# A head's value products and sums issued at the end of its own step, with priority

## The chip, the cores and the metric

The kernel runs on one core of one Trainium2 chip. The metric is the device time of one execution in microseconds (us), as the median of several runs. Names of engines: PE (TensorE, matrix products), DVE (VectorE), ACT (ScalarE), POOL (GpSimd), SP (issues DMA transfers).

## What is computed

Two layers over 512 latent tokens and 256 context tokens of width 1024, all in 32-bit floating point. Layer 0 mixes the tokens by 16 heads of attention over all 768 tokens, layer 1 by 16 heads whose latent keys are a neighbourhood of the query on a grid (and all context tokens). Behind each mixer stands a mixture of 32 experts, of which every token uses two.

```python
def attend(q, k, v):
    s = jnp.einsum('bhgqd,bhkd->bhgqk', q, k, preferred_element_type=jnp.float32)
    p = jax.nn.softmax(s, axis=-1).astype(v.dtype)
    return jnp.einsum('bhgqk,bhkd->bhgqd', p, v)

for l in range(DEPTH):                       # DEPTH = 2
    h_l = modulate(x_lat, norm_mix[l], sh1, sc1)
    h_c = modulate(x_ctx, norm_mix[l], sh1c, sc1c)
    o_c, o_l = mixer_ab(...) if l % 2 == 0 else mixer_na(...)
    x_lat = x_lat + g1 * o_l
    ...
    y = hier_moe(tokens, moe_w_rg[l], ...)   # the same for the context in layer 0
    x_lat = x_lat + g2 * y
return rmsnorm(x_lat, norm_final)
```

The shifts, scales and gates come from a product of the conditioning with w_ada, the "modulation".

## The kernel before

The time divides into four parts: projections and heads of layer 0 (27.6 to 471.3 us of the profiled execution), its experts (to 1184.7), projections and heads of layer 1 (to 1491.9), and the experts and the end (to 2108.9). The change is about the two parts with heads; the heads themselves, from the transposes of the first head's maxima on, take 164.8 to 468.5 us in layer 0 and 1264.2 to 1487.1 in layer 1.

Scores are kept transposed: a score tile holds 128 keys by 512 queries, so that its exps can be the right operand of the product with the values. In layer 0 a head has six such tiles (512 latent queries) and, on two of them, one of 128 keys by 256 context queries. Eight heads are "stacked" (a score tile takes two products, L340 and L341), eight take three (L343 to L345). In layer 1 a head has two tiles of context keys (cunit) and four of latent keys with up to 384 queries each (lunit). Before the exp the maximum of each query is subtracted: it is found a head ahead, by products and DVE reductions of their own (L286, L292 and DVE L288, L293 in layer 0; L303, L313 and DVE L307, L314 in layer 1), negated (L321, L323), transposed into a row (L326, L332) and copied by ACT into a row of the Q operand (L328, L333).

Behind the exp (ACT L356 and L361, in layer 1 L400 behind a DVE addition of the bias, L398) a tile goes two ways. The value products (L421, L425; in layer 1 L432, L438) use the exps as they are; an output of 64 columns takes half of the array, so that the products of the two halves of the queries (hf 0 and 1) run beside each other. The adds sum the exps of all tiles into acc: on POOL for tiles 1, 2 and 4 in layer 0 and for tiles c1 and 1 in layer 1, otherwise on DVE (L371 to L374, L406). When acc is whole, four products with a one-hot operand (L453, 32 columns wide, one per group of queries, beside each other) give the sums over the keys in ps_sum. At the end ACT copies the value sums into oT (L459), and a batch of heads is divided by its sums (norm_units: L491, L493).

The order is set by run_heads (L497 on). Its step i hands over, for j from 0 to 5: score tile j of head i, the maxima of head i + 1, value unit j of head i - 1, in layer 1 a piece of the projections of later heads (the filler, L1840, for i up to 12), and the add of tile j - 1; the sums of head i - 1 stand at j = 4, its ACT copy at the step's end. Step n does the value products of the last head. In layer 0 prep0 (L963, L978, L990) makes values and queries of heads to come, and extra0 calls ada_pump, that is one step of the modulation (L139: 16 products of 32 columns). A scheduler then orders each engine's instructions: it takes the order of handing over as priority and moves an instruction forward where those ahead of it aren't ready in its own model. An engine executes its list in order.

PSUM buffers: score tiles use two (ps_s), maxima and projections two (ps_a) and in layer 0 a third (ps_v); value sums are also in ps_v, sums in ps_sum. A 32-bit product is recorded twice in the trace.

## Time and profile before

| | us |
|---|---|
| median of 3 runs | 2105.77 (2102.83 to 2112.57) |
| profiled execution, its own time | 2110.64 |
| its span, first to last instruction | 2108.9 |
| PE busy | 1878.8 (89%) |
| DVE busy | 789.5 (37%) |
| ACT busy | 656.6 (31%) |
| POOL busy | 321.3 (15%) |

The mean granted clock of PE is 0.957 of full speed. The busy shares are means over parts with different limits: the experts' parts move up to 414 GB/s from memory, the parts with heads 134 and 85 GB/s on the mean. A row of the timeline has the start, the duration, the engine, the line, the operation, the names (out<-in) and shapes, and how many like it follow one another; a bracket at its end says how long the engine was idle before it and which instruction released it. PE's products overlap, so that the distance between two starts says more about the price of one than its duration.

### The profile page before, as it was taken

To read this page: it belongs to the slowest core of one execution; us is meant where nothing else is said; L and a number is where in the kernel's file an instruction comes from. 1 tells how busy PE (TensorE), PEld (TensorE's weight loads), DVE (VectorE), ACT (ScalarE), POOL (GpSimd) and SP (SyncE) were. 2 spreads that over 40 slices of the span, in tenths; PEclk is the share of its full clock that TensorE was granted. 3 is DMA by queue.
4 is the path that set the end of the run, shared out by engine and by line. 5 is a ranking of instruction groups with operands and counts; after the bars stand their busy time and mean duration, and the time that the engine had idled before them with its cause. 6 is when DMAs were issued, how large, how long until landed. Compare 5 with 4: busy or idle time off the path is not lost. (4 is left out here: it accounts for less than half of the span.)

```text
span 2108.9 us, 29478 instructions
## 1 busy us (share of the span) xinstructions
PE 1878.8 (89%) x10307; PEld 1043.7 (49%) x10308; DVE 789.5 (37%) x2041; ACT 656.6 (31%) x1462; POOL 321.3 (15%) x313
## 2 busy tenths in 40 slices
PE   7999999989969999999996999999878999978983
PEld 5886555647833333333332887676663333322321
DVE  4656676557831111111113637666760000000003
ACT  4335643442211111111112526655423222212212
POOL 0002222121011111111110101111201111111100
PEclk9999999999979999999998999999988999999997
DMA  9655321014679999699996512223578999999995
GB/s 378 217 194 209 137 94 51 5 41 158 217 296 413 414 416 380 273 390 413 414 417 242 206 43 85 73 74 132 219 269 335 412 414 414 414 414 411 413 400 191
DMA packets 96736, 563.64 MB, mean 267 GB/s; under 512 B 17446, under 2 KB 18266, under 8 KB 42928
## 3 DMA queue, kind: packets, MB, share of 16 engines
q1 hardware_dynamic: 81520, 527.41, 63.3%
q0 software_dynamic: 14912, 32.19, 4.2%
q8 instruction: 189, 3.10, 0.6%
q14 instruction: 115, 0.94, 0.1%
HBM read 543.20 MB, written 33.23 MB: 273 GB/s over the span
## 5 line engine op out<-in xcount | busy, mean ns | idle before, releaser
L1522 DVE TENSOR_TENSOR hTe<-hTe,ps_s 128x256 f32<-128x256 f32 (+1 forms) x74 | 29.9, 405 | 399.0 <-ACT hTe L1521 281.9
L1503 ACT ACTIVATE gu<-ps_a 128x512 f32<-128x512 f32 x64 | 38.2, 597 | 441.0 <-PE ps_v L1537 387.4
L1543 DVE SCALAR_TENSOR_TENSOR y<-ps_v,tg,g 128x512 f32<-128x512 f32 x32 | 24.0, 751 | 392.1 <-PE ps_v L1537 392.1
L1498 PE MATMUL ps_a<-A,xT 128*64 128x512 f32 x544 | 151.5, 602 | 5.4 <-DMA A<-in_we_dram 2.0
L1537 PE MATMUL ps_v<-wp,hTe 128*64 128x512 f32 (+1 forms) x496 | 118.0, 547 | 18.7 <-PEq L1570 17.0
L1498 PE MATMUL ps_a<-wp,xT 128*64 128x512 f32 x496 | 127.4, 594 | 1.0
L1484 ACT ACTIVATE xT<-ps_m,mods,ab 128x64 f32<-128x64 f32 x256 | 79.2, 417 | 137.9 <-PE ps_m L1477 137.9
L1544 POOL DMA_INDIRECT ybuf<-y,tab x64 | 64.7, 1012 | 330.7 <-DVEq L1583 225.4
L1840 PE MATMUL ps_v<-hT,B 128*128 128x512 f32 x384 | 102.7, 396 | 0.0
L1537 PE MATMUL ps_v<-wE,hTe 128*64 128x512 f32 (+1 forms) x352 | 90.2, 566 | 9.6 <-PEq L1570 9.6
L1498 PEld LDWEIGHTS ps_a<-A,xT 128*64 128x64 f32 x544 | 50.8, 138 | 86.9 <-issue 72.6
L356 ACT ACTIVATE pt<-ps_s 128x512 f32<-128x512 f32 x96 | 57.3, 597 | 115.1 <-PE ps_s L345 73.3
L1434 POOL DMA_INDIRECT A<-hbuf,tab x41 | 42.1, 1027 | 293.7 <-PE ps_m L1477 227.2
L1498 PEld LDWEIGHTS ps_a<-wp,xT 128*64 128x64 f32 x496 | 44.3, 137 | 72.6 <-issue 66.6
L1498 PE MATMUL ps_a<-we,xT 128*64 128x512 f32 x288 | 76.2, 595 | 3.7 <-DMA we<-in_we_dram 2.4
L1498 PE MATMUL ps_a<-wf,xT 128*64 128x512 f32 x256 | 73.7, 597 | 2.5 <-PEq L1586 0.7
L1840 PEld LDWEIGHTS ps_v<-hT,B 128*128 128x128 f32 x384 | 68.4, 188 | 12.2 <-issue 1.9
L1434 POOL DMA_INDIRECT x<-hbuf,tab x33 | 33.8, 1026 | 261.1 <-PE ps_m L1477 222.2
L1537 PEld LDWEIGHTS ps_v<-wp,hTe 128*64 128x64 f32 (+1 forms) x496 | 34.0, 129 | 73.1 <-issue 68.8
L1498 PE MATMUL ps_a<-wE,xT 128*64 128x512 f32 x240 | 64.7, 618 | 1.4 <-ACT xT L1484 0.5
L1498 PE MATMUL ps_a<-B,xT 128*64 128x512 f32 x224 | 58.9, 595 | 3.4 <-DMA B<-in_we_dram 2.4
L1537 PE MATMUL ps_v<-we,hTe 128*64 128x512 f32 x144 | 47.6, 654 | 15.8 <-PEq L1570 15.8
(556 smaller groups left out, 3816.6 us busy)
## 6 DMA issues: line engine op xcount, KB each, us to landing
wp<-in_we_dram SPq DMA_DIRECT2D x106, 1024.0 KB
A<-in_we_dram SPq DMA_DIRECT2D x84, 1024.0 KB
wE<-in_we_dram SPq DMA_DIRECT2D x62, 1024.0 KB
we<-in_we_dram SPq DMA_DIRECT2D x54, 1024.0 KB
wslot<-in_w_ada_dram SPq DMA_DIRECT2D x23, 2048.0 KB
B<-in_we_dram SPq DMA_DIRECT2D x40, 1024.0 KB
wf<-in_we_dram SPq DMA_DIRECT2D x38, 1024.0 KB
qkE<-in_wqk_dram SPq DMA_DIRECT2D x8, 1024.0 KB
```

The source lines that it names most:

```text
L356: act(h.PT[i], ps, AF.Exp, scale=h.scale)
L1434: return nc.gpsimd.indirect_dma_start(out=dst, out_offset=None, in_=S.hbuf.rearrange("n (q f) -> (n q) f", q=2), in_offset=bass.IndirectOf ...
L1484: act(xT[:, k, :], pv[:, k % 4, k // 4, :], AF.Identity, scale=ab[l][:, 1, k, 0:1], bias=mods[l][:, 24 + k, 0:1])
L1498: mm(ps[M * g:M * g + M, :N], xT[:, 4 * h + k, :M], w[:, (g * N) // 512, k, f:f + N], start=(h == 0 and k == 0), stop=(h == 1 and k == 3))
L1503: act(out[-1][:, :N], ps[:, :N], AF.Copy)
L1522: V.tensor_tensor(hv, hv, pv[:, 1], op=OP.mult)
L1537: mm(ps[M * g:M * g + M, :N], hT[:, c, :], wd[:, c, g * N:g * N + N], start=(c == 0), stop=(c == 3))
L1543: V.scalar_tensor_tensor(y[:, :N], ps[:, :N], gates[0], g2[0], op0=OP.mult, op1=OP.mult)
L1544: st = nc.gpsimd.indirect_dma_start(out=S.ybuf.rearrange("n (q f) -> (n q) f", q=n // 2), out_offset=bass.IndirectOffsetOnAxis(ap=idx, axi ...
L1840: mm(ps[:, :n], wqk[:, j, b, k, :], hT[:, a, k, c0:c0 + n], start=(k == 0 and i == 0), stop=(k == 7 and i == 2))
```

## The change

Four things change. In run_heads the loop has n steps, and the value products, the sums and the ACT copy of head i (no longer of head i - 1) are handed over at the end of step i, under `tc.high_priority()`: the scheduler takes them ahead of all else that is ready. In av_units the order of the value units is turned: layer 0 begins with tile 5, layer 1 with tiles 1 and 3, then 0 and 2, then the rest of 2 and 1, then the context tiles; the flags that start and stop the accumulation move with them. In score_units the two score tiles of the context queries go from steps 0 and 1 to steps 2 and 3, their add to step 3. In ada_pump the modulation step has high priority too. Lines below are numbered anew: 421 is 422 after, 425 426, 432 433, 438 439, 453 454, 374 375, 493 494, 963 966, 1840 1843.

```diff
--- before.py
+++ after.py
@@ -354,11 +354,11 @@
                 mm3(ps, h, i * 128, 256, 512)
                 h.PT[i] = pp.tile([128, 512], F32, name="pt", bufs=8)
                 act(h.PT[i], ps, AF.Exp, scale=h.scale)
-                if i < 2:
+                if i in (2, 3):
                     ps = P("s")
-                    mm3(ps, h, i * 128, 0, 256)
-                    h.PT["c", i] = pp.tile([128, 256], F32, name="ptc", bufs=4)
-                    act(h.PT["c", i], ps[:, :256], AF.Exp, scale=h.scale)
+                    mm3(ps, h, (i - 2) * 128, 0, 256)
+                    h.PT["c", i - 2] = pp.tile([128, 256], F32, name="ptc", bufs=4)
+                    act(h.PT["c", i - 2], ps[:, :256], AF.Exp, scale=h.scale)
 
             def two(x):
                 return x.rearrange("p (h n) -> p h n", h=2)
@@ -369,6 +369,7 @@
                     h.acc = pp.tile([128, 768], F32, name="acc", bufs=2)
                     h.accv = two(h.acc)
                     e.tensor_tensor(h.accv[:, :, 128:384], two(h.PT[0]), two(h.PT[1]), op=OP.add)
+                if i == 3:
                     V.tensor_tensor(h.accv[:, :, 0:128], two(h.PT["c", 0]), two(h.PT["c", 1]), op=OP.add)
                 if i > 1:
                     e.tensor_tensor(h.accv[:, :, 128:384], h.accv[:, :, 128:384], two(h.PT[i]), op=OP.add)
@@ -419,28 +420,28 @@
             def unit(i):
                 for hf in range(2):
                     mm(h.ps[64 * hf:64 * hf + 64, 128:384], h.V(i), h.PT[i][:, 256 * hf:256 * hf + 256],
-                       start=(i == 0), stop=(i == 5), skip_group_check=True)
+                       start=(i == 5), stop=(i == 4), skip_group_check=True)
                 if i < 2:
                     for hf in range(2):
                         mm(h.ps[64 * hf:64 * hf + 64, 0:128], h.V(i), h.PT["c", i][:, 128 * hf:128 * hf + 128],
                            start=False, stop=(i == 1), skip_group_check=True)
-            for i in range(6):
+            for i in (5, 0, 1, 2, 3, 4):
                 units.append([lambda i=i: unit(i)])
         else:
             def cunit(i):
                 for hf in range(2):
                     mm(h.ps[64 * hf:64 * hf + 64, 0:256], h.V(i), h.PT["c", i][:, 256 * hf:256 * hf + 256],
-                       start=(i == 0), stop=False, skip_group_check=True)
+                       start=False, stop=(i == 1), skip_group_check=True)
 
             def lunits(parts):
-                for j, hf, a, b, stop in parts:
+                for j, hf, a, b, start in parts:
                     q0 = max(0, j - 1) * 128
                     mm(h.ps[64 * hf:64 * hf + 64, a - 256 * hf:b - 256 * hf], h.V(2 + j),
-                       h.PT[j][:, a - q0:b - q0], start=False, stop=stop, skip_group_check=True)
-            units = [[lambda: cunit(0)], [lambda: cunit(1)],
+                       h.PT[j][:, a - q0:b - q0], start=start, stop=False, skip_group_check=True)
+            units = [[lambda: lunits([(1, 0, 0, 256, True), (3, 1, 256, 512, True)])],
                      [lambda: lunits([(0, 0, 0, 256, False), (2, 1, 256, 512, False)])],
-                     [lambda: lunits([(1, 0, 0, 256, False), (3, 1, 256, 512, False)]),
-                      lambda: lunits([(2, 0, 128, 256, True), (1, 1, 256, 384, True)])]]
+                     [lambda: lunits([(2, 0, 128, 256, False), (1, 1, 256, 384, False)])],
+                     [lambda: cunit(0)], [lambda: cunit(1)]]
         units[0].insert(0, start)
         w = 192 if h.local is None else 128
 
@@ -518,29 +519,30 @@
         norm = []
         mi[1] = 1
         vi[1] = third
-        for i in range(n + 1):
-            su, sadd = score_units(heads[i], pp) if i < n else ([], [])
+        for i in range(n):
+            su, sadd = score_units(heads[i], pp)
             mu, mf = smax_units(heads[i + 1]) if i + 1 < n else ([], None)
-            au, sums, evac = av_units(heads[i - 1], oT, pp) if i > 0 else ([], None, None)
+            au, sums, evac = av_units(heads[i], oT, pp)
             for j in range(6):
                 if j == 5 and mf:
                     mf()
                 run(su, j)
                 run(mu, j)
-                run(au, j)
                 if filler:
                     filler(i, j)
                 run(sadd, j - 1)
-                if j == 4 and sums:
-                    sums()
                 if j == 2 and norm:
                     norm.pop(0)()
             run(sadd, 5)
-            if evac:
+
+            with tc.high_priority():
+                for j in range(6):
+                    run(au, j)
+                sums()
                 evac()
-                if heads[i - 1].batch[2]:
-                    inv, *norm = norm_units(heads[i - 1].batch[0], oT, pn, pp, selh)
-                    inv()
+            if heads[i].batch[2]:
+                inv, *norm = norm_units(heads[i].batch[0], oT, pn, pp, selh)
+                inv()
             if i == 3:
                 nc.gpsimd.tensor_copy(selh, sel32[:, 0:16, None].to_broadcast([128, 16, 64]))
             if i + 2 < n:
@@ -640,7 +642,8 @@
             f()
         ada_fin.clear()
         if ada_pend:
-            ada_fin.append(ada_step(*ada_pend.pop(0)))
+            with tc.high_priority():
+                ada_fin.append(ada_step(*ada_pend.pop(0)))
         ada_ahead()
 
     pieces_g = [(0, 512), (512, 768)]
```

What stands on PE at a stacked head of layer 0 before (waits in brackets are semaphores that the instruction waits for; names as above, pt and ptc are exps, vG values, the number in front of an x the columns):

```order
L286 MATMUL ps_a<-KQ_1120,QT_1877 128x384 x2
L421 MATMUL ps_v<-pt,vG 64x256 x2
L425 MATMUL ps_v<-ptc,vG 64x128 x2
L340 MATMUL ps_s<-QT_1876,KQ_1120 128x512 [waits Activation_49]
L341 MATMUL ps_s<-QT_1876,KQ_1120 128x512
L340 MATMUL ps_s<-QT_1876,KQ_1120 128x256 [waits Activation_49]
L341 MATMUL ps_s<-QT_1876,KQ_1120 128x256
L286 MATMUL ps_v<-KQ_1120,QT_1877 128x384
L286 MATMUL ps_a<-KQ_1120,QT_1877 128x384 [waits DVE_49]
L421 MATMUL ps_v<-pt,vG 64x256 x2
L425 MATMUL ps_v<-ptc,vG 64x128 x2
```

Each score tile is followed by products of the maxima and by the value products of one tile of the head before.

The end of such a head after:

```order
L340 MATMUL ps_s<-QT_1877,KQ_1120 128x512 [waits Activation_49]
L966 MATMUL ps_v<-wv,cT 128x512 [waits DVE_49]
L422 MATMUL ps_v<-pt,vG 64x256 [waits Activation_49]
L422 MATMUL ps_v<-pt,vG 64x256 x3
L426 MATMUL ps_v<-ptc,vG 64x128 x2
L422 MATMUL ps_v<-pt,vG 64x256 x2
L426 MATMUL ps_v<-ptc,vG 64x128 x2
L422 MATMUL ps_v<-pt,vG 64x256 x6
L454 MATMUL ps_sum<-acc,ehot 32x192 [waits DVE_49]
L454 MATMUL ps_sum<-acc,ehot 32x192 x3
L326 MATMUL ps_m<-idr,nm 1x128 [waits PE_49]
L326 MATMUL ps_m<-idr,nm 1x128 x3
```

All 16 value products of the head stand in one run behind its last score tile, its sums and the transposes of the next head's maxima behind them.

DVE in a three-pass head of layer 0, from the last maxima on, before:

```order
L288 TENSOR_REDUCE mx<-ps_v 128x1 [waits PE_49]
L288 TENSOR_REDUCE mx<-ps_a 128x1 [waits PE_49]
L293 TENSOR_REDUCE mx<-ps_a 128x1 [waits PE_49]
L293 TENSOR_REDUCE mx<-ps_v 128x1 [waits PE_49]
L374 TENSOR_TENSOR acc<-acc,pt 128x2x256 [waits Activation_49,Pool_49]
L321 TENSOR_REDUCE nm<-mx 128x4 [waits DVE_49]
L323 TENSOR_SCALAR nm<-mx 128x2 [waits DVE_49]
L374 TENSOR_TENSOR acc<-acc,pt 128x2x256 [waits Activation_49,Pool_49]
```

and after:

```order
L373 TENSOR_TENSOR acc<-ptc 128x2x128 [waits Activation_49]
L375 TENSOR_TENSOR acc<-acc,pt 128x2x256 [waits Pool_49]
L375 TENSOR_TENSOR acc<-acc,pt 128x2x256 [waits Activation_49,Pool_49]
L288 TENSOR_REDUCE mx<-ps_a 128x1 [waits PE_49]
L293 TENSOR_REDUCE mx<-ps_a 128x1 [waits PE_49]
L293 TENSOR_REDUCE mx<-ps_v 128x1 [waits PE_49]
L321 TENSOR_REDUCE nm<-mx 128x4 [waits DVE_49]
L323 TENSOR_SCALAR nm<-mx 128x2 [waits DVE_49]
```

The context's add and both of DVE's latent adds have moved ahead of the last reductions (L288, L293) and of the maximum (L321, L323).

PE in a head of layer 1 from the score tile of latent tile 2 on, before:

```order
L340 MATMUL ps_s<-Q_3_16053,K_3_16054 128x384
L341 MATMUL ps_s<-Q_3_16053,K_3_16054 128x384
L1840 MATMUL ps_v<-hT_15390,B_15873 128x512 x5
L453 MATMUL ps_sum<-acc,ehot 32x128 [waits Pool_49]
L453 MATMUL ps_sum<-acc,ehot 32x128 x3
L326 MATMUL ps_m<-idr,nm 1x128 [waits DVE_49]
L326 MATMUL ps_m<-idr,nm 1x128 x3
L340 MATMUL ps_s<-Q_3_16053,K_3_16054 128x256
L341 MATMUL ps_s<-Q_3_16053,K_3_16054 128x256
```

and after, from the projections behind latent tile 1 on:

```order
L1843 MATMUL ps_v<-hT_15390,B_15873 128x512 x5
L439 MATMUL ps_v<-pt,V_15394 64x256 [waits Activation_49]
L454 MATMUL ps_sum<-acc,ehot 32x128 [waits Pool_49]
L340 MATMUL ps_s<-Q_1_16049,K_1_16050 128x384 [waits PE_49]
L341 MATMUL ps_s<-Q_1_16049,K_1_16050 128x384
L1843 MATMUL ps_v<-hT_15390,B_15873 128x512 x5
L326 MATMUL ps_m<-idr,nm 1x128 [waits DVE_49]
L326 MATMUL ps_m<-idr,nm 1x128 x2
L454 MATMUL ps_sum<-acc,ehot 32x128 [waits DVE_49]
L326 MATMUL ps_m<-idr,nm 1x128
L340 MATMUL ps_s<-Q_1_16049,K_1_16050 128x256 [waits PE_49]
L341 MATMUL ps_s<-Q_1_16049,K_1_16050 128x256
```

The first value product and the sum of group 0 stand behind latent tile 1, the sum of group 1 between the transposes; before, all four sums (of the head before) stood together.

## Rows read from the trace of the kernel before

**Rows 1.** Busy time by stretch (start:end, length), layer 0 and layer 1

```profile
core 0: us, PE busy (x) PEld busy (x) DVE busy (x) ACT busy (x) POOL busy (x), PEclk, DMA share, GB/s
164.80:283.00 118.20, 115.00 (x848) 64.72 (x845) 77.98 (x166) 67.39 (x138) 33.88 (x30) 1.00 0.48 174
...
325.40:451.60 126.20, 124.63 (x640) 75.57 (x638) 77.97 (x151) 50.05 (x103) 29.45 (x26) 1.00 0.02 7
...
1276.60:1455.70 179.10, 178.99 (x1062) 126.22 (x1063) 120.77 (x306) 102.17 (x202) 29.93 (x26) 1.00 0.24 75
```

**Rows 2.** PE's longest waits, layer 0, layer 1: us in total, times, longest us

```profile
PE ps_m L332 <- DVE nm L323: 1.7, 2, 1.0
...
PE ps_s L341 <- ACT Q L328: 1.2, 1, 1.2
```

**Rows 3.** Timeline of PE, one visit of value products in a stacked head

```profile
227.38 0.39 PE L341 MATMUL ps_s<-KQ 128*128 128x512 f32 x1
227.61 0.33 PE L286 MATMUL ps_v<-KQ,QT 128*128 128x384 f32 x1
227.78 0.34 PE L286 MATMUL ps_a<-KQ,QT 128*128 128x384 f32 x1
228.04 0.65 PE L421 MATMUL ps_v<-pt,vG 128*64 128x256 f32 x4
228.63 0.50 PE L340 MATMUL ps_s<-KQ 128*128 128x512 f32 x1
228.96 0.39 PE L341 MATMUL ps_s<-KQ 128*128 128x512 f32 x1
```

**Rows 4.** Timeline of PE, the last head of layer 0

```profile
464.92 0.51 PE L453 MATMUL ps_sum<-acc,ehot 128*32 128x192 f32 x2 [0.90 <-DVE acc L374]
465.36 0.65 PE L421 MATMUL ps_v<-pt,vM 128*64 128x256 f32 x4
...
466.71 1.47 PE L421 MATMUL ps_v<-pt,vM 128*64 128x256 f32 x12
468.11 0.53 PE L453 MATMUL ps_sum<-acc,ehot 128*32 128x192 f32 x6
468.57 0.44 PE L421 MATMUL ps_v<-pt,vM 128*64 128x256 f32 x2
```

**Rows 5.** Timeline of PE, a value product without its partner

```profile
388.25 0.65 PE L421 MATMUL ps_v<-pt,vM 128*64 128x256 f32 x2
388.82 0.38 PE L292 MATMUL ps_v<-KT,KQ 96*128 96x256 f32 x1
```

**Rows 6.** Timeline of DVE, POOL and ACT, end of a three-pass head

```profile
390.92 0.68 DVE L374 TENSOR_TENSOR acc<-acc,pt 128x512 f32<-128x512 f32 x1
...
391.75 1.28 POOL L374 TENSOR_TENSOR acc<-acc,pt 128x512 f32<-128x512 f32 x1 [7.79 <-DVE nm L323]
...
392.00 0.60 ACT L356 ACTIVATE pt<-ps_s 128x512 f32<-128x512 f32 x1 [3.15 <-PE ps_s L345]
...
392.53 0.98 ACT L459 ACTIVATE oT<-ps_v 64x384 f32<-64x384 f32 x2
...
393.06 0.69 DVE L374 TENSOR_TENSOR acc<-acc,pt 128x512 f32<-128x512 f32 x1 [1.31 <-POOL acc L374]
...
393.66 0.58 ACT L328 ACTIVATE KQ<-ps_m 1x512 fp32r<-1x512 f32 x1
```

**Rows 7.** Timeline of PE, POOL and DVE, two heads of layer 1

```profile
1301.13 0.34 PE L341 MATMUL ps_s<-Q,K 128*128 128x384 f32 x1
...
1301.65 0.87 PE L438 MATMUL ps_v<-pt,V 128*64 128x256 f32 x8
...
1302.83 1.02 POOL L406 TENSOR_TENSOR acc<-acc,pt 128x384 f32<-128x384 f32 x1 [5.59 <-ACT pt L400]
...
1317.45 0.34 PE L341 MATMUL ps_s<-Q,K 128*128 128x384 f32 x1
...
1318.88 0.43 PE L453 MATMUL ps_sum<-acc,ehot 128*32 128x128 f32 x8
1319.24 0.40 PE L326 MATMUL ps_m<-idr,nm 128*1 128x128 f32 x4
1319.32 0.56 DVE L406 TENSOR_TENSOR acc<-acc,pt 128x384 f32<-128x384 f32 x1 [0.72 <-ACT pt L400]
```

## The prediction

> **What bounds the kernel now.** I read the table of busy time by stretch first. In the two stretches that run attention heads TensorE (PE) leaves almost nothing: 115.00 of 118.20 us in layer 0's stacked heads, 124.63 of 126.20 in its three-pass heads, 178.99 of 179.10 in layer 1, all at a granted clock of 1.00 (2.4 GHz) [rows 1]. VectorE (DVE) comes next, with 120.77 of 179.10. The waits of PE say the same: the largest entry over 300 us of layer 0 is 1.7 us, the only one over layer 1's middle 1.2 [rows 2]. So the heads are bound by what PE executes in order: a saved microsecond of PE work is a saved microsecond, and an added wait of PE an added one, as there is no slack to put it in. The MoE stretches are left alone: the change moves no instruction there, so all of the difference comes from about 300 us of layer 0 (heads 0 to 15) and 220 us of layer 1.
>
> **What is there to save.** The value products are 64 columns wide (two halves side by side), the sums 32 wide (four groups side by side), all else 128. In before each unit of value products stands alone between score tiles, and the trace prices that: from one 128-wide product to the next is 0.17 us (227.61 to 227.78), from that to the first value product 0.26; four records of value products last 0.59 to the next start, where in one long run four of them take 0.47 (466.71 to 468.11 holds twelve); the 128-wide one behind takes 0.33 to its successor (228.63 to 228.96), where 0.23 stands without a change of width (227.38 to 227.61) [rows 3, 4]. That is 0.09 + 0.12 + 0.10 = 0.31 a visit, about 0.15 per change of width. Second, a product without its partner: two records cost 0.57 to the next start (388.25 to 388.82), as much as four [rows 3, 5]. So an unpaired product throws away half of a pair, 0.23. The same holds for the sums: one alone took 0.44, three together 0.46 (464.92 to 465.36, 468.11 to 468.57) [rows 4].
>
> Of the 0.31 the entry alone, 0.09, is a stretch in which no product starts; the rest shows in the products around the visit, and could be theirs for another reason. That gives the low bound, 0.05 per change, and a rival below. The Trainium skill, TensorEngine Tiling (Array Packing), Key Properties, says that a change of the tiling mode drains the TensorE, and TensorE: Matmul & The Clock Gate, Part 2 (DRAIN), gives about 128 cycles for a drain; an estimate by these is 128 / 2.4 GHz = 0.05 us per change, at the low bound, by which layer 0 would save 10 where I put 29.
>
> **Layer 0, part by part.** Counted over the built order, changes of tile width fall from 289 to 98, runs of value products from 129 to 27, and unpaired ones from 70 to 12 (eleven of them in head 0, whose products fall between those of the modulation step). 191 x 0.15 = 29 us, and 58 x 0.23 = 13 us: PE work falls by 42. The sums gain nothing (four in one run before and after). The moved context score tile and its exps are the same work in another place: 0.
>
> What comes back are waits, since in before the products of the previous head were ready long ago and filled every hole, and now they wait for their own head:
> - Entry of the clump: it starts with tile 5, whose exp lasts 0.60 (392.00's kind); score and projection products behind tile 5 cover most of it. About 0.2 for 15 heads: +3.
> - Stacked heads (7): behind the clump and the sums stand the transposes of the maxima, then ACT's copy into the Q row, 0.58, with the copy of the value sums, 0.98 for both, perhaps ahead of it [rows 6]. The old filler is used up. Per head 0.6 (the copy alone) to 1.6 (both); I take 1.1, since one product of a later head still stands in between: +8, bounds 4 and 11.
> - Three-pass heads (7 with a successor): the adds into acc become urgent. In before DVE did the last reductions of the maxima first and the last add afterwards, idle 1.31 for POOL's add of 1.28 [rows 6]. In the new order that add stands ahead of one to three reductions and of the maximum itself, so they start later by the 1.31 of idleness plus the 0.69 of the add, 2.0; L326 and then the next head's scores stand behind. The query projections (L993) between clump and L326 can hide it. Per head from 0 (hidden whole) to 3.3 (POOL's 1.28 is exposed as well); I take 2.0, as the POOL add must follow a second DVE add: +14, bounds 0 and 23.
>
> Sum of layer 0: -42 + 3 + 8 + 14 = -17; bounds -35 and -5.
>
> **Layer 1, part by part.** Changes of width fall from 186 to 121: 65 x 0.15 = -10. Unpaired products go from 28 to 32: +1. The sums are worse off: before, the four groups mostly made one run of 0.36 (1318.88 to 1319.24) [rows 7]; now group 0 stands alone behind the first value product, group 1 alone between the transposes, 2 and 3 behind the clump. A lone one costs as much as several, so two more runs of some 0.2 net of the changes already counted, in 16 heads: +6.5. PE work in all: -2.5.
>
> Now the waits. Group 0 needs POOL's add of tile 1, which ends at 1302.83 + 1.02 = 1303.85, 2.72 after that tile's last score product at 1301.13 [rows 7]. PE gets there after two maxima products, five projections and one value product: 0.52 (to 1301.65, where the value products stood) + 1.25 (1317.45 to 1318.88, less 0.18 for the score product itself) + 0.45 (0.57 less the 0.12 of an exit) = 2.2. It waits 0.5. Group 1 needs DVE's add of tile 2, ready at 1319.32 + 0.56 = 1319.88, 2.43 after 1317.45; PE is there after 1.43 (five projections, 1318.88) and three transposes (four last 0.40), 1.43 + 0.2 = 1.6, and waits 0.8. Together 1.3 a head. Nothing passes a waiting product on PE: the rest of the transposes, the next score tile, and by that its exp all stand behind it. For the 13 heads with projections +17; the last three have POOL's add right behind too, but their PE work was already short of filler: +2. From both sides: 0.75 a head (the POOL add comes half a microsecond earlier where POOL is idle) gives +7, and 1.85 in 16 heads (an add delayed by one more DVE instruction of about half a microsecond) +27. Layer 1: -2.5 + 17 + 2 = about +17.
>
> **The sum.** -17 + 17 = 0, against the profiled execution's 2110.64 us (span 2108.9), which lies within the shown runs; the same difference on the median, 2105.77, gives **2106 us**. Own range of this case -11 to +11. The modulation step (high priority too) is costed at 0: its 16 products are the same, and they stand between the same score tiles. The clock stays at 1.00, as the new pauses are about a microsecond long and PE ran at 1.00 through pauses of that size [rows 1, 2].
>
> **Rivals.**
> - Faster: the scheduler placed the new waits where other products cover them; layer 0 keeps -35 and layer 1 loses 9 only (0.75 a head, unpaired losses as above): -26, **2080**. For it: the query projections stand behind the clump in the three-pass heads, and in before the built order led to hardly a wait on PE [rows 2]. Against it: in before everything that filled the holes was a head old. It decides once the three-pass heads wait under 0.7 each.
> - Slower: the adds, not the products, set the pace. POOL's and DVE's adds into acc become a chain that in-order PE meets three times a head in layer 1, at 1.85 a head, +27; the same chain costs the three-pass heads 3.3, layer 0 then keeps -5: +22, **2128**. It decides when layer 1 waits more than (17 + 2.5) / 16 = 1.2 a head while layer 0 keeps its 17, or earlier with less. For it: 464.92, where a sum waited 0.90 for DVE's add, as the only sum that came close behind its own head [rows 4]. Against it: most adds in before idle long before they start, POOL 7.79 at 391.75 [rows 6]. The Trainium skill, TensorE: Matmul & The Clock Gate, Part 3 (The mechanism), has it that matmuls start and end strictly in order; where the 0.90 stands, the products behind it began only after it, as that says.
> - Cheap changes of width: only the entry is saved, 0.05 per change. Then layers 0 and 1 save 191 x 0.05 + 65 x 0.05 = 13 where I put 39, +26: **2132**. For it: exit and load could belong to the long streams around a visit. Against it: the load of 0.33 stands behind each visit shown, 0.23 elsewhere [rows 3]. It is the drain rule's estimate above, worked out from the entry row.
> - It doesn't do what it says: the priority could leave the order alone. The built order excludes that for layer 0 (129 runs to 27); in layer 1 "latest tile first" fails in its first product, since tile 1's half is handed over ahead of tile 3's and goes alone. Time as before, 2106.
>
> **How the numbers follow.** Forecast 0.40, faster rival 0.30, chain of adds 0.22, cheap changes 0.05, no effect 0.03. The faster case spreads some 12 us around 2080, the slower ones about as much around 2128 and 2132; leaving out about a third of each, two in ten together, gives 2076 to 2132. A measurement of this kernel can tell 0.5%, 10.5 us. Faster by more: 0.30 of the rival and a little of the forecast's edge, 0.32; slower by more: 0.27 of two rivals and the other edge, 0.29; the rest 0.39.
>
> **What would show it.** In the profile of after: PE busy in layer 0's heads lower by about 40, layer 0's heads shorter by about 17; PE waits of the sums (L454) for POOL and for DVE acc in layer 1, about 0.5 and 0.8 in each of 13 heads, layer 1 longer by about 17; DVE adds (L375) that idle for POOL with reductions behind. If L454 shows no waits in layer 1, or L326 and the maxima none in layer 0, the faster rival holds. If PE's busy time in layer 0 falls by 23 only, the changes of width are cheap. If the stretches outside the heads move, I have missed something.

## The result, and the profile after

The changed kernel takes 2126.86 us in the median of four runs (2125.88 to 2130.08), the kernel before 2106.84 beside it: a ratio of 1.0097, 95% interval 1.0083 to 1.0112. It is 20 us slower. That lies in the predicted range (2076 to 2132) and within 2 us of the rival "slower" (2128); the case that was held likeliest, no measurable change, did not come. As the experiments show, the 20 us are not that rival's; that the time lies so near to it is chance.

The table of busy time by stretch tells where the 20 us are. Its columns are those of [rows 1]; the stretches are now the heads of layer 0 and of layer 1 as a whole, from the first transpose of maxima (L326) to the end of the last sum. Of before:

```profile
164.80:468.60 303.80, 296.70 (x1855) 173.61 (x1852) 191.63 (x380) 142.68 (x291) 76.73 (x68) 1.00 0.26 91
1264.20:1487.10 222.90, 221.00 (x1311) 151.96 (x1309) 149.62 (x384) 125.84 (x252) 40.54 (x36) 1.00 0.28 90
```

Of after:

```profile
177.50:469.90 292.40, 271.63 (x1857) 173.70 (x1854) 186.64 (x380) 143.66 (x292) 77.30 (x68) 0.99 0.27 93
1264.70:1507.50 242.80, 224.22 (x1311) 157.91 (x1309) 153.94 (x386) 125.75 (x251) 40.09 (x36) 1.00 0.26 85
```

Three things are to be seen. The heads of layer 0 are 11.4 us shorter and PE is busy 25.1 us less in them. They begin 12.7 us later, though (177.5 for 164.8), so that layer 0 gains nothing. And the heads of layer 1 are 19.9 us longer: PE idles 18.6 us there in place of 1.9, and works 3.2 us more. The sum, -11.4 + 12.7 + 19.9 = 21, is the difference of the spans (2128.4 to 2108.9) within 2 us.

**The late start.** It lies in the projections of layer 0, of which the prediction has only a sentence. The timeline of PE between two tiles of projections, in before:

```profile
63.87 1.93 PE L139 MATMUL ps_m<-wslot,cs 128*32 128x256 f32 x32
65.74 2.05 PE L214 MATMUL ps_v<-x 128*128 128x128 f32 x16
```

and in after (the last row is of a later such place):

```profile
66.01 0.51 PE L148 MATMUL ps_m<-sel,mp 128*128 128x4 f32 x4
...
68.96 2.08 PE L214 MATMUL ps_v<-x 128*128 128x128 f32 x8 [2.44 <-ACT ht_t L225]
...
74.20 3.64 PE L139 MATMUL ps_m<-wslot,cs 128*32 128x256 f32 x32 [3.16 <-DMA wslot<-in_w_ada_dram]
77.77 1.74 PE L214 MATMUL ps_v<-x 128*128 128x128 f32 x8
...
115.44 2.61 PE L139 MATMUL ps_m<-wslot,cs 128*32 128x256 f32 x32 [2.48 <-ACT mp L141]
```

The stretch of after around 74 us by busy time and granted clock (the third column from the end):

```profile
72.00:74.20 2.20, 0.00 (x1) 0.03 (x2) 1.70 (x8) 1.74 (x7) 0.00 (x0) 0.50 1.04 447
74.20:77.70 3.50, 3.50 (x32) 1.54 (x32) 1.82 (x8) 1.00 (x4) 0.00 (x0) 0.50 0.66 281
```

The modulation step (L139) stands at the head of PE's queue, and its weights haven't landed: PE waits 3.16 us for the transfer, with the DMA engines full. The 2.44 us ahead of it, in front of L214, are another wait. They are for ACT's copy (L225), which stands behind DVE, and DVE stands behind a transfer of its own (L761, 10.15 us; the same operation of before, L758, waits 10.6, but there PE had the step at 63.87 to do meanwhile). Where this wait is missing, in e2 below, the modulation step waits 5.20 us and starts at nearly the same time, 74.65: the landing of its weights sets the end of the pause in both. Behind the pauses the granted clock is 0.50 (1.2 GHz), so that the 32 records last 3.6 us, where the step at 63.87 in before took 1.93 at full clock; and no step of before between 50 us and the first head waited for a transfer. A second pause follows at 112.96 (2.48 us, for ACT's copy of the step before). It is no wait for weights, as the expectation of e2 below has it.

From 50 us to the first head PE idles 8.1 us in after and 1.0 in before, and is busy 119.4 us for 113.8, at a mean granted clock of 0.95 for 1.00. So 7 of the 12.7 us are waiting and the rest is slower work.

**Layer 1.** The waits of PE in the heads of layer 1, after (line waited for and releaser; us in total, times, longest):

```profile
PE ps_sum L454 <- POOL acc L407: 7.1, 16, 0.9
PE ps_sum L454 <- DVE acc L407: 5.3, 9, 0.6
PE ps_a L303 <- DVE mx L307: 3.6, 8, 0.5
```

Of the first two before has a single wait, of 0.2 us. One head in the timeline of PE and DVE, to be held against [rows 7], where one run of eight records followed the projections without a wait:

```profile
1308.73 0.41 PE L454 MATMUL ps_sum<-acc,ehot 128*32 128x128 f32 x2 [0.42 <-POOL acc L407]
...
1310.67 0.34 PE L326 MATMUL ps_m<-idr,nm 128*1 128x128 f32 x3
1311.00 0.56 DVE L407 TENSOR_TENSOR acc<-acc,pt 128x384 f32<-128x384 f32 x1 [0.72 <-ACT pt L401]
1311.62 0.41 PE L454 MATMUL ps_sum<-acc,ehot 128*32 128x128 f32 x2 [0.60 <-DVE acc L407]
1311.95 0.22 PE L326 MATMUL ps_m<-idr,nm 128*1 128x128 f32 x1
```

The fourth transpose stands behind a sum that waits for DVE's add; ACT's copy into the Q row, and with it the next head's scores, come behind that transpose.

### The profile page after: what moved, and what is told of

It reads as the page before. It is cut to its first block, busy times and chain, and to the rows that moved or that the text cites. A ratio compares the mean times of both kernels' runs of the same rounds, so it can differ in the third digit from the quotient of the medians.

```text
span 2128.4 us, 29440 instructions
## 1 busy us (share of the span) xinstructions
PE 1858.8 (87%) x10307; PEld 1044.4 (49%) x10308; DVE 790.1 (37%) x2041; ACT 657.0 (31%) x1462; POOL 321.5 (15%) x313
## 5 line engine op out<-in xcount | busy, mean ns | idle before, releaser
L139 PE MATMUL ps_m<-wslot,cs 128*32 128x256 f32 x736 | 57.2, 426 | 16.9 <-DMA wslot<-in_w_ada_dram 13.4
```

Source lines behind the costliest of these rows:

```text
L139: i = mm(ps[32 * g:32 * g + 32, 0:256], cs[:, k, :], w[:, k, 256 * h:256 * h + 256], start=(k < 2), stop=(k > 5))
```

## The experiments

Each is timed in three rounds beside the kernel before (2108.4 to 2109.6 in these, so that differences between kernels of different rounds are uncertain by about 1 us besides). "Layer 0's heads" and "layer 1's heads" are the two stretches above. Counts of changes of tile width, runs of value products and unpaired ones are from the built order, all counted in one way here, which gives 298 changes for layer 0 before and 102 after, where the prediction had 289 and 98.

### The modulation's priority alone

e1_no_ada is the changed kernel without its last hunk:

```diff
         if ada_pend:
-            with tc.high_priority():
-                ada_fin.append(ada_step(*ada_pend.pop(0)))
+            ada_fin.append(ada_step(*ada_pend.pop(0)))
```

> The changed kernel with the modulation step at ordinary priority, as in the kernel before; all else as changed. Theory (three places that add up: projections of layer 0 +12.7 us by the modulation's priority, heads of layer 0 -12.5, heads of layer 1 +19.9): the projections end at 165 again instead of 177.5 and the time falls by 12 to 13, to about 2114. Rival (the delay in the projections comes from elsewhere, the priority only moved the waits): within 4 us of the changed kernel, 2123 to 2127.

Measured: 2108.41 us, ratio 1.000 (0.9986 to 1.0014), that is 18.5 less than the changed kernel and level with the kernel before beside it. More than was expected: the heads begin at 165.4 again, and besides layer 0's heads are 282.5 us long, 10 shorter than in after:

```profile
165.40:447.90 282.50, 261.58 (x1857) 171.35 (x1854) 186.64 (x380) 143.55 (x292) 77.20 (x68) 0.99 0.27 97
```

Layer 1's stay at 242.7.

e2_ada_only makes that hunk in the kernel before and nothing else.

> The kernel before with the modulation step alone at high priority. Theory: PE reaches the modulation products before their weights have landed, as at 74.2 and 115.4 us of the changed kernel, and its clock falls to half behind each pause: 10 to 14 us slower than before, about 2119. Rival (the pauses need the whole change): within 4 us of before, 2103 to 2111.

Measured: 2121.03, ratio 1.0064 (1.0041 to 1.0086), 12.6 us slower. Its timeline of PE has the same pause:

```profile
74.65 3.22 PE L139 MATMUL ps_m<-wslot,cs 128*32 128x256 f32 x32 [5.20 <-DMA wslot<-in_w_ada_dram]
```

and its heads are those of before (303.7 us, beginning at 177.1). So the 12.7 us are the priority's alone. The 10 us inside layer 0's heads come only with both parts. Two kernels tell these apart: e13_ada_proj keeps the priority in the changed kernel only for the calls between the projection tiles, e14_ada_mid only for the two calls ahead of the heads.

```diff
-    def ada_pump():
+    def ada_pump(high=False):
...
-        if ada_pend:
+        if ada_pend and high:
             with tc.high_priority():
                 ada_fin.append(ada_step(*ada_pend.pop(0)))
+        elif ada_pend:
+            ada_fin.append(ada_step(*ada_pend.pop(0)))
...
-    ada_pump()
-    ada_pump()
+    ada_pump(True)
+    ada_pump(True)
```

(e14; e13 has `ada_pump(True)` at the call between projection tiles instead.)

> The changed kernel with the modulation step's priority kept only for the calls between the projection tiles of layer 0; the two calls ahead of the heads and those within them have ordinary priority. Theory (the priority costs at two places that add up: 12.7 us where PE waits for the modulation's weights between projections, some 10 in head 0): only the first is paid, 12 to 13 us slower than e1_no_ada, about 2121. Rival (one cause: the late projections shift head 0 as well): 2125 to 2128 as the changed kernel.

> The changed kernel with the modulation step's priority kept only for the two calls ahead of layer 0's heads. In the built order head 0's value products then alternate with modulation products, in 12 runs instead of one. Theory (two places that add up): 8 to 11 us slower than e1_no_ada, 2116 to 2119, with head 0 at 30 us instead of 21. Rival (the alternation costs little and head 0 was slow by its late start): within 4 us of e1, 2108 to 2112.

Measured: e13 2120.14, 11.7 over e1; e14 2116.71, 8.3 over e1. Both are near the theory of two places, and together 20 for the 18.5 between e1 and after (held each against the kernel before of its own round, 10.5 and 7.1 for 20.0). In e14 the heads begin at 164.9, so a late start isn't what slows head 0:

```profile
164.90:457.30 292.40, 271.61 (x1857) 173.52 (x1854) 186.66 (x380) 143.68 (x292) 77.16 (x68) 0.99 0.26 94
```

Head 0 lasts 31.2 us in place of 21.1 in e1, as in after. The timeline of PE in e14 shows most of the reason:

```profile
182.13 1.05 PE L139 MATMUL ps_m<-wslot,cs 128*32 128x256 f32 x10
...
187.50 0.62 PE L139 MATMUL ps_m<-wslot,cs 128*32 128x256 f32 x2
188.05 0.43 PE L426 MATMUL ps_v<-ptc,vG 128*64 128x128 f32 x2
188.41 0.62 PE L139 MATMUL ps_m<-wslot,cs 128*32 128x256 f32 x2
188.96 0.43 PE L426 MATMUL ps_v<-ptc,vG 128*64 128x128 f32 x2
189.32 0.62 PE L139 MATMUL ps_m<-wslot,cs 128*32 128x256 f32 x2
189.87 0.65 PE L422 MATMUL ps_v<-pt,vG 128*64 128x256 f32 x2
190.45 0.62 PE L139 MATMUL ps_m<-wslot,cs 128*32 128x256 f32 x2
191.00 0.65 PE L422 MATMUL ps_v<-pt,vG 128*64 128x256 f32 x2
...
196.07 0.28 PE L326 MATMUL ps_m<-idr,nm 128*1 128x128 f32 x2
```

The same products in e1, in runs:

```profile
180.93 1.05 PE L139 MATMUL ps_m<-wslot,cs 128*32 128x256 f32 x10
...
185.09 1.50 PE L139 MATMUL ps_m<-wslot,cs 128*32 128x256 f32 x22
186.51 0.34 PE L326 MATMUL ps_m<-idr,nm 128*1 128x128 f32 x3
```

In e14 modulation and value products, both of high priority, alternate one by one. A modulation product of 256 columns and a value product of as many cost 1.12 us together (189.32 to 190.45). In runs a value product is 0.23 [rows 4] and a modulation product 0.12 (before has 16 in 1.87, from 63.87 to 65.74). Eleven such pairs lose 11 x (1.05 - 0.3) = 8 us, with 1.05 and 0.3 as means over long and short pairs; from 182.13 to 196.07 against 180.93 to 186.51 it is 8.4. The other 1.6 us of head 0 are the clock's, in its first modulation step (after, then e1):

```profile
181.22 3.52 PE L139 MATMUL ps_m<-wslot,cs 128*32 128x256 f32 x32
...
169.07 1.93 PE L139 MATMUL ps_m<-wslot,cs 128*32 128x256 f32 x32
```

The granted clock is 0.53 there in after and 1.00 in e1. The priority isn't the reason: e3 below, without it, takes 3.51 us for this step, and e13 takes 1.94.

### Each layer alone

e3_l0_only has the clump (a head's value products in one piece at the end of its own step), its order and the moved context tiles in layer 0 only, e4_l1_only the clump in layer 1 only; the modulation step as before in both. Run_heads takes the new or the old way by layer:

```diff
-        for i in range(n + 1):
+        new = NEW[heads[0].local is not None]
+        for i in range(n + (not new)):
...
+            d = i if new else i - 1
+            au, sums, evac = av_units(heads[d], oT, pp) if d >= 0 else ([], None, None)
...
-                run(au, j)
+                if not new:
+                    run(au, j)
...
+            if new:
+                with tc.high_priority():
+                    for j in range(6):
+                        run(au, j)
+                    sums()
+                    evac()
...
```

> The clump, its order and the moved context tiles in layer 0 only; layer 1 and the modulation step as before. Theory: the gain of layer 0's heads stands alone, 12 to 14 us faster than before, about 2093. Rival (layer 0 gained only because its heads began late and found their weights and transfers ready): 0 to 5 us faster, 2102 to 2107.

> The clump in layer 1 only; layer 0 and the modulation step as before. Theory: the whole loss of layer 1's heads, 19 to 21 us slower than before, about 2127. Rival (a part of layer 1's loss comes from the state that layer 0 leaves behind): under 14 slower.

Measured: e3 2086.15, ratio 0.9899 (0.9878 to 0.992), 22.3 us faster than before; e4 2128.81, ratio 1.0104 (1.0083 to 1.0126), 20.4 slower. The layers don't disturb each other: -22.3 + 20.4 = -1.9, and e1 with both stands at 0.0. e3's gain is larger than the theory's 12 to 14, because head 0 isn't torn apart, as e14 shows. In the busy time of e3's heads,

```profile
164.60:447.20 282.60, 261.68 (x1857) 171.26 (x1854) 186.82 (x380) 143.58 (x292) 77.24 (x68) 0.99 0.27 97
```

PE works 35.0 us less than before, and idles 20.9 in place of 7.1. All the added waits are single ones of at most 1.2 us; the most frequent are the clump's for the last exp and the score tiles' for a free buffer:

```profile
PE ps_v L424 <- ACT pt L358: 3.5, 9, 0.7
PE ps_s L343 <- ACT pt L358: 3.3, 9, 0.4
```

### What layer 1 pays for

Three kernels start from e4. e5_l1_sums_low takes the sums out of the priority:

```diff
                 with tc.high_priority():
                     for j in range(6):
                         run(au, j)
-                    sums()
                     evac()
+                sums()
```

e6_l1_order lets the first value unit begin with tile 3's half, so that no product goes ahead of the rest; e9_l1_both has both edits.

```diff
-            units = [[lambda: lunits([(1, 0, 0, 256, True), (3, 1, 256, 512, True)])],
+            units = [[lambda: lunits([(3, 1, 256, 512, True), (1, 0, 0, 256, True)])],
```

> Layer 1's clump alone (as e4_l1_only, 20 us slower than before), but its sums handed over behind the clump at ordinary priority, so that the order puts projections ahead of them again. Theory (the split sums cost layer 1 its time: PE waits 7.1 + 5.3 us for the adds, and three runs instead of one): 14 to 18 us faster than e4, 2111 to 2115. Rival (the clump itself costs: the value products are no longer there to fill the holes between the maxima): 2121 to 2129.

> As e4_l1_only, but the first value unit hands over tile 3's half ahead of tile 1's, so that all ten value products stand in one run; the sums stay at high priority and split. Theory (the lone product costs an unpaired place, two of 0.23 us a head, and a visit of about 0.2, in 16 heads; the sums' waits stay): 4 to 10 us faster than e4, 2119 to 2125. Rival (the lone product was the cause of most of the loss, since it pulled the sum of group 0 along): 2115 or less.

> e5's and e6's edits together: layer 1 with one run of ten value products a head, one or two visits of the sums behind ordinary work, changes of width in layer 1 from 186 to 65. Theory (without the sums' waits the changes of width count): PE work falls by 121 changes of 0.1 to 0.15 and 28 unpaired products of 0.23, some 18 to 24 us, of which waits for the last exp and the next score tile take back 0.6 a head: 5 to 14 us faster than before, 2094 to 2103. Rival (the holes between the maxima must be filled by value products): slower than before, 2109 to 2118.

Measured: e5 2112.75, ratio 1.0013 (0.9998 to 1.0028), 16 us faster than e4, as the theory of the sums had it. Layer 1's heads are 226.7 us for e4's 243.0, with less work than in before (221.00) but 6.8 us of idleness:

```profile
1270.00:1496.70 226.70, 219.90 (x1310) 157.07 (x1308) 149.59 (x386) 125.15 (x251) 40.02 (x36) 0.99 0.28 91
```

e6 2125.74 (1.0087), 3 faster than e4: just short of the theory's low end, and the lone product isn't the cause. e9 2114.05 (1.0018) is no faster than e5: its theory (2094 to 2103) fell, and the time is its rival's (2109 to 2118). Its layer 1 and the waits in it say what happened:

```profile
1265.60:1493.70 228.10, 212.47 (x1311) 156.85 (x1309) 148.33 (x386) 125.49 (x251) 40.50 (x36) 0.97 0.28 90
```

```profile
PE ps_sum L455 <- POOL acc L408: 4.3, 3, 1.6
PE ps_s L340 <- ACT ptc L385: 2.9, 6, 0.5
PE ps_v L440 <- ACT pt L402: 2.7, 7, 0.5
PE ps_a L303 <- DVE K L247: 2.1, 4, 0.5
```

PE works 8.5 us less than in before and idles 15.6 in place of 1.9. The clump waits for its last exp, score tiles for a buffer, maxima for the K of a head to come: the products that stood between these were gone. In the last 34 us the granted clock is 0.85 besides: twelve records of value products (L440) take 2.1 to 2.2 us in the last three heads for 1.13 in the one before (1458.37 to 1459.50), and the slow products of the three together cost some 4 us. At the prices found below, 121 changes of width and 28 unpaired products less would be 18 us of work; with the 4 added back it is 12.5, and the rest isn't accounted for. So the sums' place is 16 of layer 1's 20 us; the rest, and all that fewer changes of width could give, goes to holes that the value products of the head before used to fill.

e8_l0_new_l1_prev and e11_l0_new_l1_prev0 check that from the other side. They keep e3's layer 0 and give layer 1 the value products and sums of the head before (i - 1, all long ready) in one piece, without priority, behind score tile 1 (e8) or 0 (e11). Against e3, e8 is:

```diff
-                if not new:
-                    run(au, j)
+                if j == 1 and sums and not new:
+                    for k in range(6):
+                        run(au, k)
+                    sums()
...
-                if j == 4 and sums and not new:
-                    sums()
```

> Layer 0 as changed (e3_l0_only, 2086), layer 1 with the value products and the sums of the head before in one piece behind score tile 1, at ordinary priority: all that they need is long ready, so no wait is added. Theory (changes of width cost 0.1 to 0.15 each whatever the waits): 83 fewer changes, 7 to 12 us faster than e3, 2074 to 2079. Rival (the products were needed as filler between the maxima, which now wait for DVE): 2086 to 2095.

> As e8_l0_new_l1_prev (2083), but layer 1's products and sums of the head before stand behind score tile 0 instead of tile 1: 85 changes of width there instead of 103, 20 unpaired products instead of 28. Theory (the built order's counts carry over where nothing waits): 18 x 0.13 + 8 x 0.23 = 4 us faster than e8, about 2078. Rival (so close behind the head before, the sums wait for the last add): as e8 or slower, 2083 to 2090.

Measured: e8 2082.81, ratio 0.9865 (0.9834 to 0.9897); e11 2081.46, ratio 0.9875 (0.9856 to 0.9893). Layer 1's heads in e8:

```profile
1247.30:1462.20 214.90, 210.37 (x1311) 155.06 (x1309) 149.03 (x384) 123.82 (x253) 40.38 (x36) 1.00 0.29 93
```

and in e11:

```profile
1241.00:1454.90 213.90, 207.78 (x1311) 155.64 (x1309) 149.46 (x384) 124.47 (x252) 40.59 (x36) 0.99 0.29 94
```

They are 8 and 9 us shorter than before, with 103 and 85 changes of width for 186. In the whole time only 3 to 5 us of it show beyond e3 (4.5 and 5.9 if each is held against the kernel before of its own round), less than the 7 to 12 expected of e8; PE's work fell by 10.5 and the waits rose by 2.6. In the profiled execution of e8 the part behind layer 1's heads took 624.5 us (2086.7 - 1462.2), in that of e3 618.5 and in that of e11 622.3; a difference between executions is enough for that, as after, e13 and e14, whose layer 1 is the same, take 617.6 to 622.7 there. e11 isn't told apart from e8, and its theory (2078) isn't reached. Both beat the two kernels given.

### The price of a change of width

e10_l0_tile_order is e3 with the value units in the order of the tiles: the priority then sends each off as soon as its tile is there.

```diff
-                       start=(i == 5), stop=(i == 4), skip_group_check=True)
+                       start=(i == 0), stop=(i == 5), skip_group_check=True)
...
-            for i in (5, 0, 1, 2, 3, 4):
+            for i in range(6):
```

> As e3_l0_only (22 us faster than before), but layer 0's value units in the order of the tiles, 0 to 5, so that the priority lets them go as soon as their tile is there: 69 runs of value products instead of 16, 196 changes of width instead of 83, no unpaired product in either. Theory (a change of width costs some 0.13 us, as PE's busy time in e8's layer 1 has it): 113 changes, 12 to 17 us slower than e3, 2098 to 2104. Rival (cheap changes, 0.05: the gain of layer 0 came from the pairs): 3 to 8 us slower, 2089 to 2095.

Measured: 2100.0 us, ratio 0.9955 (0.9939 to 0.9972), 13.9 slower than e3, in the theory's 12 to 17.

```profile
164.80:458.60 293.80, 275.79 (x1856) 164.72 (x1854) 189.42 (x380) 144.29 (x294) 76.71 (x68) 1.00 0.26 90
```

PE works 14.1 us more than in e3 with 113 more changes of width and no unpaired product in either: 0.125 us per change. Layer 1 of e8 against e3, at the same number of unpaired products: 220.91 - 210.37 = 10.5 for 83 changes, 0.127. The two agree. Against before e10 has 102 changes and 70 unpaired products less and 20.9 us less work: 20.9 - 102 x 0.125 = 8.1, or 0.12 per unpaired product by busy time. It also shows what the order "latest tile first" does: the high priority alone doesn't make a run, since the scheduler lets every product that is ready go (69 runs of value products for 16); the product that waits for the last tile holds the others back.

## Why the prediction came out as it did

The time is in the range by chance: what the prediction added up, two layers that cancel, came out as it said (e1), and 20 us came on top from a step that it had put at 0. Step by step:

**The modulation step, costed at 0: the step that failed.** "its 16 products are the same, and they stand between the same score tiles" looked at the products, not at what they wait for, nor at the stretch before the heads. e1 puts it at 18.5 us: 12.6 in the projections (e2), where a step of high priority stood on PE ahead of its weights' landing and the clock fell, and 8 in head 0 (e14), where two kinds of high-priority products alternate. The clue was in the prediction: "eleven of them in head 0, whose products fall between those of the modulation step" stands there as a count; the value products among them were priced as unpaired, the modulation products that lose their partners were not. Without this the forecast of 2106 would have been met: e1 measures 2108.41, the kernel before 2108.41.

**"The clock stays at 1.00".** Wrong in the projections: 0.50 from 72 to 77.7 us. Wrong in a small way in layer 0's heads too, where the pauses are the short ones that it spoke of: 0.53 from 181.2 to 184.7 and 0.50 from 277 to 280, some 1.5 us each. It held in layer 1's heads of after (1.00), where the pauses were 1.2 us at most.

**Layer 0's PE work, -42.** In e1 and e3, free of the modulation's priority, PE's busy time is 35 lower, with 215 changes and 70 unpaired products less. By busy time the price of a change was near (0.15 put, 0.125 measured) and that of an unpaired product too high (0.23 put, 0.12 measured). But the prediction priced products from start to start, and in front of a wait busy time is more than that: a product of 512 columns is busy for 0.39 us, while in a row the next one starts after 0.23 [rows 3]. An estimate from the starts in the traces gives each product in front of a wait the usual distance of its kind to the next start, and the rest to the wait. By it e3's layer 0 works 38 to 44 us less than that of before and waits 17 to 23 more (the lower figures if pauses under 0.15 us aren't counted as waits); a change costs 0.13 to 0.14 and an unpaired product 0.12 to 0.21. So the -42 was right as far as can be told, and whether 0.23 was too high stays open. The low bound of 0.05, and with it the rival of cheap changes, is refuted by e10 either way. The Trainium skill, TensorEngine Tiling (Array Packing), Key Properties, says that a change of the tiling mode drains the TensorE; e10 and e8 agree that a change costs, at 0.125 us, more than twice the 0.05 that the prediction estimated from the skill's pages. That it is a drain no run here shows.

**Layer 0's waits, +25.** By idle time +13.8 in e3 (20.9 for 7.1), by the estimate above 17 to 23: the size is near, but the places are mostly not those named. The adds of the three-pass heads did hold DVE; its waits for POOL from the first of these heads on, before and after:

```profile
DVE acc L374 <- POOL acc L374: 5.2, 4, 1.3
DVE acc L375 <- POOL acc L375: 10.0, 7, 1.5
```

They didn't reach PE: no sum (L454) of layer 0 waited for an add, and the maxima lost little, as the products of projections stood in between, which the prediction had named as the cover and then counted for 1.3 of 3.3 us a head. ACT's copy into the Q row, put at +8 for the stacked heads, shows as 3.1 us in four waits of L332. What PE waited for most was exps and free score buffers. The net in e3, -21, is near the forecast's -17; that other waits than those named add up to about as much is luck.

**Layer 1, +17.** Measured +19.9. The waits for the adds were put at 0.5 and 0.8 a head; the trace has 0.44 in 16 heads for POOL and 0.6 in nine for DVE, 12.4 us for the 19 of the sum (17 and 2). PE's work was put at -2.5; by busy time it is +3.2, by the estimate from starts -1 to -2, with 21 to 22 us of added waits. The split sums account for their term: from start to start, waits left out, the sums take 15.0 us in after and 7.4 in before, +7.6 for the +6.5 put. The changes of width were to give 10: the value products take 4.7 less (43.7 for 48.4), and the products of 128 columns, whose slower first one behind a run was part of the price, 1.8 less (159.4 for 161.2), or 11 in all by the estimate. A wait of the maxima for their buffer (3.6 us in eight heads) wasn't foreseen. e5 shows that the sums' place was the greater part.

**The rivals.** "Slower: the chain of adds" met the time, and in layer 1 its mechanism, at the forecast's price rather than its own: 0.8 a head of waiting for the adds, below the 1.2 from which it was to decide. It would not have decided alone, since e1 with all of that loss is level with before. The remaining 20 us are the modulation's. "Faster" came near for layer 0 alone, without the modulation's priority (e3: 22 us of the 35 that it kept there), and only there.

## What to carry to other kernels

Price a priority by what the instruction waits for, everywhere it is given: an in-order engine that meets a step ahead of its weights pays the wait, and the slower clock behind it. Gathering narrow products is worth what the count of width changes says (0.125 us each here) only while what they leave still gets filled; products of the head before, all ready, can be gathered with little waiting (2.6 us more in all of e8's layer 1), while those of the own head wait for their last input. Don't give two kinds of narrow products the same high priority at the same place, and don't let a reduction's last product become urgent before the chain of adds that feeds it is done.

## What the runs showed of the hardware that was not expected

A product of 32 columns and one of 64 that alternate cost 1.12 us a pair, where in runs of each the two cost 0.35 (e14, 189.32 to 190.45; before, 63.87 to 65.74 and [rows 4]). Each of the two takes as long there as a product without a partner: 0.55 and 0.58 from start to start, for the 0.57 of the lone one of [rows 5].

The granted clock fell behind the pause of 2.44 us already: the eight records of L214 at 68.96 take 2.08 us, in e2, where a pause of 0.30 stands ahead of them, 1.16. It was 0.50 from 72.0 to 77.7 us, though PE was busy for the last 3.5 of them. Pauses below 1 us didn't always leave it at 1.00 either. Head 0 begins with pauses of 0.34, 0.17 and 0.74 us in after, e1, e3 and e13 alike; the modulation step behind them takes 3.52 us (after) and 3.51 (e3), but 1.93 (e1) and 1.94 (e13). In layer 1's heads of after, with pauses of up to 1.2 us, the clock stayed at 1.00; in the last 34 us of e9's, with pauses of up to 1.65, it was 0.85.
